# One inference step of a hybrid decoder: the prompt's compressed keys and values join the other key blocks

## Chip, cores and metric

The kernel runs on one core of a Trainium2 chip. The metric is the device time of one execution in microseconds (us); before the change it is 1101.69 us, the median of three runs (1101.4 to 1104.07). The engines are named as in the profile: PE (TensorE, matmuls) with PEld (its weight loads), DVE (VectorE), ACT (ScalarE), POOL (GpSimd), SP (SyncE, which issues most DMAs).

## The reference

One layer with two head groups is computed for a prompt of 1024 tokens and for 8 decode samples. An input projection (1024 to 4384 columns) feeds 4 mLSTM heads of 128 and 8 attention heads of 64 with 2 shared key/value heads. Each attention head has three branches, merged by gates. The change concerns the prompt's first branch, the compressed one, and the sum over all three:

```python
def nsa_prompt(qa, cmp_rows, slc_rows, win_rows, ga, cmp_params, rel_bias):
    kc = compress(cmp_rows, *cmp_params)            # 63 compressed keys and values per KV head
    o_c, imp = cmp_attend(q, kc, t_pos, rel_bias)   # softmax over the compressed keys
    ...
    o_w = window_prompt(q, win_rows, rel_bias)      # keys of the last 512 positions
    return gate_merge(ga, o_c, o_s, o_w)            # g0*o_c + g1*o_s + g2*o_w
```

`compress` takes windows of 32 positions with a step of 16: two halves of 16 positions, each times its half of `w1`, are added to a bias; GELU, then `w2`, for keys and for values. In the second branch the 16 selected blocks of 64 are all there are, so `o_s` runs over all earlier keys.

The output projection, a residual and a layer norm follow, and several caches and states are outputs too.

## The kernel before

Everything is emitted by generators ("lanes") with a rank. A planner (`Plan`, `Lanes`) keeps a modelled clock for each engine; at each turn the lane of lowest rank whose operands its model holds to be ready emits its next step. So the order of instructions on each engine is fixed when the program is built, and each engine works in that order. All of this is recorded through one helper, which is why every row of the profile has line L281; tiles tell the rows apart.

- Projections (`mm`): three float32r matmuls (`hh`x`wh`, `hl`x`wh`, `hh`x`wl`) per 128 input rows and 344 tokens. Their lane has the highest rank number, 9, so they fill PE wherever no other lane is ready.
- `kv_done` (L1158) takes a projected key or value tensor. For the compressed branch it copies it into `xtp`, with even positions on partitions 0 to 63 and odd ones on 64 to 127 (L1168 to 1178).
- `prompt_compress` (L1211): matmuls `sc<-xtp,w1f` read `xtp` through a view with a step of 8 elements, then GELU, then the compressed keys `kcp` and values `vcp`. The flag "pcmp" at its end starts the loads of the decode samples' selected keys (L1410) and is one of those that the attention waits for (L1968).
- `key_stacks` (L1832): keys are held as a float32r high part on 64 partitions and the remainder on the other 64. The selected keys go to `KS_` (tile `kst`, 1024 columns), the window's to `KW`, the compressed ones to `KC` (tile `kcs`).
- Attention works in 32 units: 2 KV heads x 8 query blocks of 128 x 2 pairs of heads. A unit with query block qb has nb = qb + 1 blocks of selected keys and min(nb, 5) of the window. `Unit.scores` (L2006) makes the logits of each of the unit's two heads in chunks of up to 512 columns (`score_chunks`, L1977): `qs` and `ql` are the high and low parts of the query, each a stationary operand for one matmul. In the first chunk the 64 compressed columns and the selected columns are two separate pairs of matmuls. DVE adds biases and finds minima, ACT takes exponentials into `pa` and `pw` (`pp` for nb up to 3; the compressed ones stand behind the window's in `pw`).
- `Unit.values` (L2104): blocks of 128 probabilities of both heads are scaled, transposed on PE (`tp`), copied from PSUM to a tile `pt` by ACT or DVE, and multiplied with the values (`oo<-pt,VT`), in groups of two blocks. A product has a stationary operand of 64 columns and goes to PSUM rows 0 to 63 for one head and 64 to 127 for the other. The compressed block is a group of its own, of 64 columns (`oo<-pt,vcp`). Products run LAG = 2 groups behind the transposes:

```python
                if len(pend) > LAG:
                    yield [pend[0][0]]
                    product(*pend.pop(0))
            while pend:
                yield [pend[0][0]]
                product(*pend.pop(0))
```

- Behind the last unit's values ("values") start the output gate, the samples' mLSTM (L1651) and the loads and splits of the output weights (L2273). The output projection comes last.

Of the kernel before, what the change touches and what calls it, by code (L numbers as in the profile page):

```python
# [9 lines left out]
F32R = mybir.dt.float32r  # L10
I32 = mybir.dt.int32
AF = mybir.ActivationFunctionType
ALU = mybir.AluOpType
# [314 lines left out]
def build(ctx, tc, I, O, dbg=None):  # L328
# [13 lines left out]
    def R(shape, name, dt=F32):  # L342
        return rp.tile(shape, dt, name=name, tag="R", bufs=NR)
# [811 lines left out]
    xtp = []  # L1155
    outs_kv = {0: ("cmp_p", "cmp_s"), 1: ("slc_p", "slc_s"), 2: ("win_p", None)}

    def kv_done(br, s, f):  # L1158
# [9 lines left out]
        if br == 0:  # L1168
            x = R([128, 2, 512], "xtp")
            fv = f[:, 0:SEQ].rearrange("p (n two) -> p two n", two=2)  # L1170
            for p2 in range(2):
                for kv in range(2):
                    o, i_ = x[64 * p2:64 * p2 + 64, kv], fv[64 * kv:64 * kv + 64, p2]
                    if kv:
                        S.activation(o, i_, AF.Copy)
                    else:
                        V.tensor_copy(o, i_)
            xtp.append(x)
# [29 lines left out]
    kcp = C([128, 2, 64], "kcp")  # L1208
    vcp = C([64, 2, 64], "vcp")

    def prompt_compress():  # L1211
# [5 lines left out]
        for c in range(2):  # L1217
            r = slice(64 * c, 64 * c + 64)
            ps = yield from bank("sc")
            xr = xtp[c].rearrange("p k (n a) -> p a k n", a=8)  # L1220
            for a in range(8):
                T.matmul(ps[:, 0:128], w1[c][:, a].rearrange("p j h -> p (j h)"), xr[:, a], start=(a == 0),
                         stop=(a == 7))
            S.activation(tm[r].rearrange("p k n -> p (k n)"), ps[64:128, 0:128], AF.Identity, bias=cst[r])
            V.tensor_tensor(x[r, :, 0:63], ps[0:64, 0:128].rearrange("p (k n) -> p k n", k=2)[:, :, 0:63],
                            tm[r, :, 1:64], op=ALU.add)
            yield
# [9 lines left out]
        for kv in range(2):  # L1237
            T.matmul(ps[0:64, 64 * kv:64 * kv + 64], x[64:128, kv], w2[64:128], start=True, stop=True)
        V.tensor_scalar(vcp.rearrange("p k e -> p (k e)"), ps[0:64, 0:128], 0.5, None, op0=ALU.mult)
        yield  # L1240
# [591 lines left out]
    def key_stacks(kv):  # L1832

        r = slice(64 * kv, 64 * kv + 64)
        KS_[kv], KW[kv] = [R([128, SEQ], "kst", F32R) for _ in range(2)]
        if not KC:
            KC.append(H([128, 2, 64], "kcs", F32R))
            stack(KC[0], kcp)
        VT[kv] = R([128, 2, 8, 64], "VT")
        near_bias(kv)  # L1840
        for t in range(2):
            m = slice(512 * t, 512 * t + 512)
            for i, k in enumerate((KS_[kv], KW[kv])):
# [3 lines left out]
                yield [a]  # L1847
                stack(k[:, m], a)
                if t == 0:
# [146 lines left out]
    class Unit:  # L1996
# [9 lines left out]
        def scores(self):  # L2006
# [9 lines left out]
            for g in range(2):  # L2016
# [13 lines left out]
                for i, (c0, c1) in enumerate(ca):  # L2030
                    ps = yield from bank("sc", True)
                    n = c1 - c0
                    s0 = max(c0, 64)
                    if i == 0:
                        product(ps[:, 0:64], KC[0][:, kv])
                    product(ps[:, s0 - c0:n], KS_[kv][:, s0 - 64:c1 - 64])
                    if i == 0:
# [66 lines left out]
        def values(self):  # L2104
# [6 lines left out]
            chunks += [(self.PW, c0, c1, 2, x) for x, (c0, c1) in enumerate(cw)]  # L2111
            groups = [[(self.PW, oc, 64, vcp[:, kv], 0)]]
            blocks = []
            for k, (P, c0, c1, br, x) in enumerate(chunks[1:], 1):
                for o in range(c0, c1, 128):
                    i = o // 128 + (nb - nbw if br == 2 else 0)
                    blocks.append((P, o, 128, VT[kv][:, br - 1, i], k))
            groups += [blocks[i:i + 2] for i in range(0, len(blocks), 2)]
            scaled = [0]
# [25 lines left out]
            for group in groups:  # L2145
# [9 lines left out]
                pend.append((pt, group))  # L2155
                if len(pend) > LAG:
                    yield [pend[0][0]]
                    product(*pend.pop(0))
            while pend:
                yield [pend[0][0]]  # L2160
                product(*pend.pop(0))
# [290 lines left out]
```

## Time and profile before

| | |
|---|---|
| median of three runs | 1101.69 us |
| the profiled execution | 1101.59 us, its span 1099.8 us |
| PE busy | 1009.0 us (92%), 7445 records |
| PEld busy | 884.3 us (80%) |
| DVE, ACT, POOL busy | 724.9, 525.2, 289.3 us |
| granted TensorE clock, mean | 0.966 of full speed |
| PE's share of the chain that ended last | 69%, DVE 17% |

How to read it: a float32 matmul or product appears as two records, a float32r one and a transpose as one. Matmuls are pipelined and their ends are modelled, so the length of a PE record is not what it costs; that is the distance to the next start, and for weight loads as well. "issue" is idle time in which an engine waited for nothing that the profile shows.

### The profile page before, as it was taken

How to read it: one execution, taken by the hardware profiler on the slowest of the kernel's cores; microseconds unless marked ns; L12 is line 12 of the kernel's file. 1: busy time of each engine (PE TensorE's matmuls, PEld its weight loads, DVE VectorE, ACT ScalarE, POOL GpSimd, SP SyncE). 2: the span in 40 equal slices, each digit the busy share in tenths (PEclk: the TensorE clock that was granted, in tenths of full speed). 3: DMA queues.
4: the chain of work that ended last, by engine and by line, in shares of the span. 5: the costliest groups of instructions: out<-in, count | busy, mean ns of one | idle time of the engine just before them, and what ended most of it. 6: DMA issues, size and time to landing. Idle time of an engine off the chain costs nothing.

```text
span 1099.8 us, 20348 instructions
## 1 busy us (share of the span) xinstructions
PE 1009.0 (92%) x7445; PEld 884.3 (80%) x7445; DVE 724.9 (66%) x2285; ACT 525.2 (48%) x1313; POOL 289.3 (26%) x363
## 2 busy tenths in 40 slices
PE   6898699999798999999999999999999999989991
PEld 5787698888675789889889888888888898867780
DVE  4678962252212446778787777878776757898996
ACT  4466662242243556666566676766774223231211
POOL 6315421111633111010113000111001533443463
PEclk9798899999899999999999999999999999989996
DMA  9953406504855753321002311011110515479512
GB/s 309 411 192 98 154 25 245 166 21 134 312 194 191 251 165 101 111 85 54 25 26 89 83 43 35 23 37 64 44 42 20 172 40 139 124 257 351 192 41 78
DMA packets 124750, 141.45 MB, mean 129 GB/s; under 512 B 21049, under 2 KB 102564, under 8 KB 124522
## 3 DMA queue, kind: packets, MB, share of 16 engines
q1 hardware_dynamic: 115434, 106.59, 30.9%
q0 software_dynamic: 9216, 33.56, 8.4%
q8 instruction: 59, 0.97, 0.4%
q14 instruction: 41, 0.34, 0.1%
HBM read 117.73 MB, written 28.15 MB: 133 GB/s over the span
## 4 chain that ended last, share of the span: by engine, by line
PE 69%; DVE 17%; issue 4%; DMA 3%; ACT 2%; POOL 2%; another core or an unknown queue 1%; SPq 1%; POOLq 0%; DVEq 0%; ACTq 0%
PE mm L281 30%; PE sc L281 17%; PE tp L281 13%; PE oo L281 8%; DMA wada<-in_w_ada 2%; DVE xr L281 2%; DVE rs_t L281 1%; SPq L281 1%; DVE lnst L281 1%; DVE smp L281 1%; DVE mixl L281 1%; DVE nd L281 1%; DVE tot L281 1%; DVE rs_y L281 1%
## 5 line engine op out<-in xcount | busy, mean ns | idle before, releaser
L281 PE MATMUL mm<-hh,wh 128*128 128x344 f32 (+1 forms) x840 | 285.9, 341 | 1.1 <-DVE pa L281 0.8
L281 PE MATMUL mm<-hl,wh 128*128 128x344 f32 (+1 forms) x840 | 269.8, 321 | 0.0
L281 PE MATMUL mm<-hh,wl 128*128 128x344 f32 x816 | 262.1, 321 | 0.0
L281 POOL TENSOR_TENSOR wl<-wf,wh 128x1024 fp32r<-128x1024 f32 (+1 forms) x35 | 83.0, 2372 | 498.7 <-ACT wh L281 343.6
L281 PEld LDWEIGHTS mm<-hh,wh 128*128 128x128 f32 (+1 forms) x840 | 158.3, 188 | 15.2 <-issue 10.8
L281 PEld LDWEIGHTS mm<-hl,wh 128*128 128x128 f32 (+1 forms) x840 | 158.5, 189 | 0.5
L281 PEld LDWEIGHTS mm<-hh,wl 128*128 128x128 f32 x816 | 154.7, 190 | 0.0
L281 PE MATMUL oo<-pt,VT 128*64 128x128 f32 x1056 | 78.0, 281 | 1.2 <-DVE pt L281 1.2
L281 ACT ACTIVATE pt<-tp 128x512 f32<-128x512 f32 (+2 forms) x88 | 46.6, 531 | 60.3 <-PE tp L281 59.6
L281 PE MATMUL sc<-kst,qs 128*128 128x384 f32 (+3 forms) x208 | 71.7, 350 | 0.6 <-ACT ti L281 0.5
L281 PEld LDWEIGHTS oo<-pt,VT 128*64 128x64 f32 x1056 | 55.7, 136 | 17.4 <-issue 10.2
L281 DVE COPY pt<-tp 128x512 f32<-128x512 f32 (+1 forms) x80 | 50.1, 635 | 25.8 <-PE tp L281 25.8
L281 PE MATMUL sc<-kst,ql 128*128 128x384 f32 (+3 forms) x208 | 63.8, 315 | 0.0
L281 ACT ACTIVATE pa<-pa,nbs 128x384 f32<-128x384 f32 (+1 forms) x88 | 51.0, 581 | 24.1 <-DVE pa L281 22.1
L281 ACT ACTIVATE xh<-tp 128x512 fp32r<-128x512 f32 x64 | 37.6, 595 | 47.6 <-PE tp L281 43.1
L281 ACT ACTIVATE pw<-pw,nbs 128x64 f32<-128x64 f32 (+2 forms) x112 | 54.6, 488 | 10.5 <-DVE nbs L281 5.4
L281 DVE TENSOR_TENSOR xl<-tp,xh 128x512 fp32r<-128x512 f32 x64 | 43.1, 683 | 21.3 <-ACT xh L281 16.8
L281 PE MATMUL tp<-KA,pgx 128*128 128x128 f32 x256 | 44.4, 301 | 6.7 <-issue 4.2
L281 PE MATMUL sc<-xl,w1h 128*128 128x256 f32 x128 | 39.6, 310 | 11.1 <-DVE xl L281 11.1
L281 PE MATMUL sc<-xh,w1h 128*128 128x256 f32 x128 | 44.5, 347 | 0.7 <-ACT xh L281 0.7
L281 ACT ACTIVATE ti<-sc,PKT 128x129 f32<-128x129 f32 x28 | 10.4, 371 | 70.2 <-DVE cx L281 70.2
L281 ACT ACTIVATE ktT<-tp 128x512 f32<-128x512 f32 x40 | 22.1, 596 | 44.8 <-PE tp L281 32.9
(509 smaller groups left out, 2377.7 us busy)
## 6 DMA issues: line engine op xcount, KB each, us to landing
wf<-in_w_in SPq DMA_DIRECT2D x34, 512.0 KB
wada<-in_w_ada SPq DMA_DIRECT2D x24, 512.0 KB
wof<-in_w_out SPq DMA_DIRECT2D x16, 512.0 KB
xt<-in_x_prompt SPq DMA_DIRECT2D x8, 512.0 KB
pgs<-in_cache_win_kv SPq DMA_DIRECT2D x8, 512.0 KB
qf<-qtd SPq DMA_DIRECT2D x32, 128.0 KB
mix<-mxd SPq DMA_DIRECT2D x16, 256.0 KB
mix<-gtd SPq DMA_DIRECT2D x16, 256.0 KB
```

The source lines that it names most:

```text
L281: return f(*a, **kw)
```

## The change

`xtp` is stored in the order in which it is read. `vcp` becomes 128 rows, with the values in the upper 64 and zeros below. The compressed keys stand in columns 0 to 63 of `kst` and the selected ones behind them; the last 56 of these, which don't fit in its 1032 columns, stay in `kcs`.

```diff
@@ kv_done
-            x = R([128, 2, 512], "xtp")
-            fv = f[:, 0:SEQ].rearrange("p (n two) -> p two n", two=2)
+            x = R([128, 8, 2, 64], "xtp")
+            fv = f[:, 0:SEQ].rearrange("p (n a two) -> p two a n", a=8, two=2)
...
-                    o, i_ = x[64 * p2:64 * p2 + 64, kv], fv[64 * kv:64 * kv + 64, p2]
+                    o, i_ = x[64 * p2:64 * p2 + 64, :, kv], fv[64 * kv:64 * kv + 64, p2]
@@ prompt_compress
-    vcp = C([64, 2, 64], "vcp")
+    vcp = C([128, 2, 64], "vcp")
...
-            xr = xtp[c].rearrange("p k (n a) -> p a k n", a=8)
+            xr = xtp[c].rearrange("p a k n -> p a (k n)")
...
-            T.matmul(ps[0:64, 64 * kv:64 * kv + 64], x[64:128, kv], w2[64:128], start=True, stop=True)
-        V.tensor_scalar(vcp.rearrange("p k e -> p (k e)"), ps[0:64, 0:128], 0.5, None, op0=ALU.mult)
+            T.matmul(ps[64:128, 64 * kv:64 * kv + 64], x[64:128, kv], w2[64:128], start=True, stop=True)
+
+        V.memset(vcp[0:64], 0.0)
+        V.tensor_scalar(vcp[64:128].rearrange("p k e -> p (k e)"), ps[64:128, 0:128], 0.5, None, op0=ALU.mult)
@@ key_stacks
-        KS_[kv], KW[kv] = [R([128, SEQ], "kst", F32R) for _ in range(2)]
+        KS_[kv], KW[kv] = R([128, NT], "kst", F32R), R([128, SEQ], "kst", F32R)
         if not KC:
-            KC.append(H([128, 2, 64], "kcs", F32R))
-            stack(KC[0], kcp)
+            KC.append(H([128, 2, SEQ + 64 - NT], "kcs", F32R))
+        stack(KS_[kv][:, 0:64], kcp[:, kv])
...
-                stack(k[:, m], a)
+                if i == 0:
+                    o = 64 + 512 * t
+                    n = min(512, NT - o)
+                    stack(k[:, o:o + n], a[:, 0:n])
+                    if n < 512:
+                        stack(KC[0][:, kv], a[:, n:512])
+                else:
+                    stack(k[:, m], a)
@@ Unit.scores
-                    if i == 0:
-                        product(ps[:, 0:64], KC[0][:, kv])
-                    product(ps[:, s0 - c0:n], KS_[kv][:, s0 - 64:c1 - 64])
+                    e = min(c1, NT)
+                    product(ps[:, 0:e - c0], KS_[kv][:, c0:e])
+                    if c1 > e:
+                        product(ps[:, e - c0:n], KC[0][:, kv])
@@ Unit.values
-            groups = [[(self.PW, oc, 64, vcp[:, kv], 0)]]
-            blocks = []
+            blocks = [(self.PW, oc - 64, 128, vcp[:, kv], 0)]
...
-            groups += [blocks[i:i + 2] for i in range(0, len(blocks), 2)]
+            groups = [blocks[i:i + 2] for i in range(0, len(blocks), 2)]
...
-                if len(pend) > LAG:
-                    yield [pend[0][0]]
+                if len(pend) > LAG + 1:
+                    yield [pend[1][0]]
                     product(*pend.pop(0))
+                    product(*pend.pop(0))
+            yield [x[0] for x in pend]
             while pend:
-                yield [pend[0][0]]
                 product(*pend.pop(0))
```

The compressed block is now 128 columns wide: its lower 64 are the last columns of the window's block beside it, which meet the zeros of `vcp`. It is the first of the unit's blocks, and these go in groups of two throughout. Products start when four groups are pending and then go two groups at a time; at the end all that is left goes together.

The order on PE in a unit's values, for a unit with nb = 6 (12 blocks). `pa` and `pw` are probabilities, `nd` belongs to the mLSTM. Before:

```order
L281 MATMUL oo<-pt,vcp 64x128 x2
L281 MATMUL tp<-KA,pa 128x128 x4
L281 MATMUL oo<-pt,VT 64x128 x4
L281 MATMUL tp<-KA,pw 128x128 x4
L281 MATMUL oo<-pt,VT 64x128 x4
L281 MATMUL tp<-KA,pw 128x128 x4
L281 MATMUL oo<-pt,VT 64x128 x4
L281 MATMUL tp<-KA,pw 128x128 x2
L281 MATMUL oo<-pt,VT 64x128 x10
L281 MATMUL tp<-KA,nd 128x128 x4
```

And after, for a unit of the same size, with the mLSTM's (`vx`, `cx`) and the next scores (`kst`) behind it:

```order
L281 MATMUL tp<-KA,pw 128x128 x2
L281 MATMUL oo<-pt,vcp 64x128 x2
L281 MATMUL oo<-pt,VT 64x128 x6
L281 MATMUL tp<-KA,pw 128x128 x8
L281 MATMUL oo<-pt,VT 64x128 x16
L281 MATMUL sc<-vx,kw 128x129
L281 MATMUL sc<-cx,qm 128x129
L281 MATMUL sc<-vx,wt 128x129
L281 MATMUL sc<-kst,qs 128x448
L281 MATMUL sc<-kst,ql 128x448
```

The same 24 products stand in two runs where there were five.

The order on PE in the scores of one head with nb = 8 (`vm` belongs to the mLSTM). Before:

```order
L281 MATMUL sc<-kcs,qs 128x64
L281 MATMUL sc<-kcs,ql 128x64
L281 MATMUL sc<-kst,qs 128x384
L281 MATMUL sc<-kst,ql 128x384
L281 MATMUL tp<-KA,pw 64x128 x2
L281 MATMUL tp<-KA,pa 128x128 x4
L281 MATMUL tp<-KA,vm 128x128 x4
L281 MATMUL sc<-kst,qs 128x384
L281 MATMUL sc<-kst,ql 128x384
L281 MATMUL sc<-kst,qs 128x256
L281 MATMUL sc<-kst,ql 128x256
```

After:

```order
L281 MATMUL sc<-kst,qs 128x448
L281 MATMUL sc<-kst,ql 128x448
L281 MATMUL tp<-KA,pw 128x128 x2
L281 MATMUL tp<-KA,pa 128x128 x2
L281 MATMUL sc<-kst,qs 128x384
L281 MATMUL sc<-kst,ql 128x384
L281 MATMUL sc<-kst,qs 128x200
L281 MATMUL sc<-kst,ql 128x200
L281 MATMUL sc<-kcs,qs 128x56
L281 MATMUL sc<-kcs,ql 128x56
```

The pair of 64 columns is gone from the first chunk, which has 448 now, and in this largest size a pair of 56 columns has come at the end of the third; the transposes of 64 columns (`tp<-KA,pw 64x128`) are gone too.

## Rows read from the trace of the kernel before

**Rows 1.** The windows view over four stretches of the span: the stretch in us, its length, busy us and instructions of PE, PEld, DVE, ACT and POOL, the granted clock, the DMA share and GB/s.

```profile
260.00:385.00 125.00, 108.65 (x866) 87.94 (x866) 34.41 (x73) 46.61 (x90) 39.87 (x36) 0.96 0.64 216
385.00:850.00 465.00, 456.99 (x3755) 403.38 (x3754) 343.37 (x1441) 302.18 (x911) 62.56 (x145) 1.00 0.21 61
850.00:975.00 125.00, 116.88 (x785) 108.71 (x784) 91.81 (x237) 32.76 (x67) 49.55 (x64) 0.99 0.44 131
975.00:1100.00 125.00, 96.88 (x444) 75.86 (x442) 109.22 (x199) 24.09 (x29) 57.45 (x28) 0.89 0.54 177
```

**Rows 2.** The waits of PE between 385 and 850 us: who waited for whom, us in total, times, the longest; the first, second and last of eight.

```profile
PE tp L281 <- DVE pp L281: 2.9, 3, 1.4
PE oo L281 <- DVE pt L281: 1.2, 1, 1.2
...
PE tp L281 <- DVE kw L281: 0.2, 1, 0.2
```

**Rows 3.** The same view for PEld: the four with "issue".

```profile
PEld oo L281 <- issue: 15.0, 86, 0.4
PEld tp L281 <- issue: 10.6, 54, 1.5
PEld mm L281 <- issue: 6.7, 39, 0.2
PEld sc L281 <- issue: 4.3, 21, 0.3
```

**Rows 4.** PE in order of time, in the attention: start in us, length, engine, line, operation, tiles, shape of the stationary operand, shape of what is streamed, records merged. Left out are the `ql` matmuls, each of the width of the `qs` before it, and one more pair of 256.

```profile
657.86 0.34 PE L281 MATMUL sc<-kst,qs 128*128 128x384 f32 x1
...
658.21 0.28 PE L281 MATMUL sc<-kst,qs 128*128 128x256 f32 x1
...
658.44 0.34 PE L281 MATMUL sc<-kst,qs 128*128 128x384 f32 x1
...
659.12 0.66 PE L281 MATMUL oo<-pt,VT 128*64 128x128 f32 x8
659.71 0.66 PE L281 MATMUL tp<-KA,pw 128*128 128x128 f32 x4
660.30 0.66 PE L281 MATMUL oo<-pt,VT 128*64 128x128 f32 x8
660.89 0.43 PE L281 MATMUL mm<-hh,wh 128*128 128x344 f32 x1
```

**Rows 5.** The same view at two more places: a long run of products, and six transposes (the two of the compressed block, 64 columns wide, come first; the form shown is theirs).

```profile
665.32 1.31 PE L281 MATMUL oo<-pt,VT 128*64 128x128 f32 x20
666.56 0.43 PE L281 MATMUL mm<-hh,wh 128*128 128x344 f32 x1
...
847.02 0.82 PE L281 MATMUL tp<-KA,pp 128*64 128x128 f32 x6
847.59 0.40 PE L281 MATMUL mm<-hh,wh 128*128 128x344 f32 x1
```

**Rows 6.** The chain of waits between 255 and 300 us, in order of time: start, us, what. `sc` x16 are the matmuls on `xtp`.

```profile
259.07 0.44 PE tp L281 x4
259.51 0.95 PE mm L281 x6
260.46 3.72 PE sc L281 x16
...
265.57 3.73 PE sc L281 x16
...
275.78 12.50 another core or an unknown queue
```

**Rows 7.** The tile `kcs`: count, shortest/median/longest in ns, first and last start in us, form. The rows for `ql` are as many.

```profile
L281 PE MATMUL sc<-kcs,qs x64: 191/193/277, 385.8 to 832.6; 128*128 128x64 f32 x64
...
L281 ACT ACTIVATE kcs<-kcp x1: 298/298/298, 361.6 to 361.6; 128x128 fp32r<-128x128 f32 x1
L281 DVE TENSOR_TENSOR kcs<-kcp,kcs x1: 2377/2377/2377, 361.9 to 361.9; 64x128 fp32r<-64x128 f32 x1
```

**Rows 8.** PEld in order of time, at the first head's scores.

```profile
385.80 0.19 PEld L281 LDWEIGHTS sc<-kcs,ql 128*128 128x128 f32 x1
385.91 0.19 PEld L281 LDWEIGHTS sc<-kst,qs 128*128 128x128 f32 x1
386.02 0.19 PEld L281 LDWEIGHTS sc<-kst,ql 128*128 128x128 f32 x1
```

**Rows 9.** PE in order of time, at float32 matmuls of the mLSTM whose streamed operand lies in adjacent columns.

```profile
853.04 1.05 PE L281 MATMUL sc<-qm,km 128*128 128x128 f32 x8
853.85 0.41 PE L281 MATMUL mm<-hh,wh 128*128 128x344 f32 x1
```

**Rows 10.** The tiles `tp`, `xtp` and `oo`, columns as in rows 7: the copies to `pt`, the copies to `xtp`, and the products.

```profile
L281 ACT ACTIVATE pt<-tp x88: 363/593/600, 420.1 to 847.4; 128x512 f32<-128x512 f32 x63, 64x256 f32<-64x256 f32 x18, 128x256 f32<-128x256 f32 x7
L281 DVE COPY pt<-tp x80: 406/684/693, 430.4 to 847.9; 128x512 f32<-128x512 f32 x65, 64x256 f32<-64x256 f32 x14, 128x256 f32<-128x256 f32 x1
...
L281 ACT ACTIVATE xtp<-kvf x4: 659/668/672, 231.8 to 247.1; 64x512 f32<-64x512 f32 x4
L281 DVE COPY xtp<-kvf x4: 406/420/422, 234.0 to 246.8; 64x512 f32<-64x512 f32 x4
...
L281 PE MATMUL oo<-pt,VT x1056: 272/273/324, 423.9 to 849.5; 128*64 128x128 f32 x176
```

## Prediction

> **What bounds the kernel now.** I read the stretches first, then who waits for whom inside the attention, then the order of time on TensorE (PE). Four stretches, cut by what PE does [rows 1]: up to 385 us projections and the decode samples' keys; 385 to 850 us the prompt's attention, with projection matmuls as filler; 850 to 975 us the rest of the projections with the mLSTM; then the output projection. In the attention PE is busy 457.0 of 465 us, DVE 343.4, ACT 302.2, at a granted clock of 1.00. All that PE waits there for another engine is eight groups of 2.9 down to 0.2 us, 7.8 us together [rows 2]. So PE's instruction stream sets the pace of 465 us, and any time taken out of it should come off. After 975 us it is different: DVE is busy 109.2 of 125 us and PE 96.9.
>
> PE's busy time hides something, though. The weight loads (PEld) stand idle with nothing to wait for ("issue") 86 times before a product `oo`, 54 times before a transpose `tp`, 39 before a projection `mm` and 21 before a score `sc`: 36.6 us for 200 times, 0.18 us each [rows 3]. The order of time shows where. A run of eight `oo` records (two blocks of keys) takes 0.59 us to the next start, one of twenty takes 1.24 [rows 4, 5]. The twelve more cost 0.65, so a record costs 0.054, eight cost 0.43, and 0.16 us belongs to the run, however long. Four transposes followed by a product take 0.59 us [rows 4]; in the chain of waits four take 0.44 [rows 6]; 0.15 more. One excursion into the value products so costs about 0.16 + 0.15 = 0.31 us beside its work. What differs is the shape: a product's stationary operand has 64 columns and writes 64 output rows, all around it work on 128.
>
> **The change part by part.**
>
> *Value products in twos.* In the order of the two programs I counted the uninterrupted runs of rows that write `oo` from `pt`: 120 before, 63 after. The rule in the code gives nearly that: a unit with G groups makes one run per group beyond two, and one flush (108 over all units; other lanes split some); now one per two groups beyond three, and a flush (60). 57 fewer excursions at 0.31 are 17.7 us. Bounds: 0.16 us if only one side of a run is really paid (9.1), and twice the mean idle of 0.183 (20.9). I take 0.31, which is read from the runs themselves. The compressed keys' products also stop being a shape of their own (64 rows instead of 128), which I count at nothing beyond the runs.
>
> *Scores.* There are 64 head units (32 units of 2 heads), and each loses one narrow matmul for `qs` and one for `ql` [rows 7]. In the weight loads everything up to 128 columns follows at 0.11 us [rows 8]: 128 x 0.11 = 14.1 us. The first chunk of each head becomes 64 columns wider. Two matmuls of 384 columns take 0.35 us and two of 256 take 0.23 [rows 4], so 64 columns are 0.03 us; 112 matmuls pay it (3.4 us), and the 16 that go from 128 to 192 columns stay at the 0.11. The eight heads with eight blocks get two more matmuls of 56 columns, because the keys end at column 1032: 16 x 0.11 = 1.8, less 0.1 for their 256 that become 200. Net 14.1 - 3.4 - 1.7 = 9.0 us. Bounds: 12.4 if the wider ones cost nothing more; 5.6 if each of the 112 pays the whole step of 0.06 us between 256 and 384 columns.
>
> *Compress.* Two sets of sixteen matmul records read `xtp` with a step of 32 bytes and take 3.72 and 3.73 us on the chain [rows 6]; eight records of the same size that read adjacent columns take 0.81 us [rows 9], so sixteen take 1.62. 2 x 2.1 = 4.2 us. Both stand on the chain, and behind them come the gathers of the samples' keys (12.5 us of a queue, same rows), which start when `kcp` and `vcp` are written; they move up with it. Bounds 0 and 4.2; I take 4.2. The other side of this edit are the eight copies that fill `xtp`, 0.42 us on DVE and 0.67 on ACT now [rows 10]. They read with a step of 64 bytes instead of 8. The nearest row for a strided read is PE's own, 3.72 against 1.62, a factor of 2.3: 4 x (0.55 + 0.87) = 5.7 us more on two engines under full projection work. The cover is the `mm` filler; the bounds are 0 and 5.7, and I take 0.
>
> The Trainium skill has a rule on this, in "SBUF — State Buffer", the note on SBUF lines in the section on the DMA port swizzle: reads that leave a 16-byte line at each element lose bandwidth. By it `xtp` read contiguously gains, as the factor shows, and the copies, now at 64 bytes, lose, which speaks against the change; this is the second rival below.
>
> *What is added.* One memset of half of `vcp`; three more pieces for the key stacks in all (an ACT and a DVE instruction each; the widest seen, for `kcp`, took 0.30 and 2.38 us [rows 7]) in front of or under filler work: 0 to 5 us, taken as 0. The compressed transposes become 128 wide. In the trace six transposes of which two are 64 wide go in 0.57 us [rows 5], like full ones, so nothing changes. Eight copies of `pt` fewer, 0.59 or 0.68 us each [rows 10], on engines that are not waited for: 0. In units of up to three blocks the first transposes now also wait for the scaling of the window's columns: 12 units with up to 0.4 us; queued behind them is the filler, which comes first where they aren't ready. I take 1 us.
>
> *What is late next.* PE walks through the attention some 6% faster, against the same DVE and ACT work: 343 of about 438 us is 78%. The 7.8 us of waits [rows 2] should grow; I take 3 us, bounds 0 and 8. In the order, 480 projection matmuls stand behind the last product, before it was 510; the 30 at 0.158 us (0.95 us for six, [rows 6]), 4.7 us, go ahead of it. In total PE work this is nothing, but the last stretches have idle PE time (116.9 of 125 busy), so part of it isn't won back: 1.5 us, bounds 0 and 4.7.
>
> **Sum.** -17.7 - 9.0 - 4.2 + 1 + 3 + 1.5 = -25.4 us. The profiled execution took 1101.59 us (span 1099.8), which is the median of the runs (1101.69) within 0.1; 1101.6 - 25.4 = 1076. What follows the attention starts at the flag of the last unit (gate, samples' mLSTM, output weights), so it moves with it.
>
> The Trainium skill states in "TensorEngine Tiling (Array Packing)", Key Properties, that changing the tiling mode drains the engine. Our products' boundaries fit that. Taken by the letter it holds for the 64-column transposes too, and the change removes 32 runs of these, another 10 us: 1066. The row of six transposes shows no such cost.
>
> **Rivals.**
> - *64-column transposes pay as well*: 32 runs x 0.31 = 9.9 us more won, 1066. Against it: the 0.57 us for six [rows 5]. Chance 5%.
> - *The copies into `xtp` are slow and uncovered*: 5.7 us later, 1082. For it: the factor of 2.3 on PE. Against it: DVE and ACT are behind `mm` work there, which doesn't read `xtp`. Chance 5%.
> - *DVE or ACT become the bound* in the attention. If half of its 26.7 us is lost to waits (in place of the 3 us), it is -13.3 - 4.2 + 2.5 = -15 us, 1087. For it: DVE ends the longest of PE's present waits. Against it: all of these are 7.8 us. Chance 12%.
> - *The excursion's cost is of each block, not of the run*, so putting runs together saves nothing: -9.0 - 4.2 + 5.5 = -7.7 us, 1094. Against it: 1.24 us for twenty records, 0.59 for eight. Chance 5%.
> - *The change doesn't reach the end*: what follows the attention takes up what it wins, and the kernel stays at 1100. For it: PE has idle time there, 8.1 and 28.1 of 125 us [rows 1]. Against it: all of it waits for the last unit's flag or for projections. Chance 4%.
> - *Slower*: PE works in order, and a flush now needs the copies of up to three groups at once. If each of the 63 runs waits for its last copy, 0.6 us [rows 10], that is 38 us: -25.4 + 38 = +12.6, 1114. It decides from 25.4 / 63 = 0.40 us per run. For it: such a wait was there once, 1.2 us [rows 2]. Against it: by the spacings above, each group's products stand at least 1.1 us of PE work behind its last transpose in the new order, median 2.8 (before 0.7 and 2.0). Chance 4%.
>
> **How the numbers follow.** The forecast has 65%; its own ends are 20.9, 12.4 and 4.2 us won with no loss (1064), and 9.1 in place of 17.7 for the runs (1085). The range 1064 to 1091 takes in the first three rivals with room above the third, and leaves out the last three, 13%, and the forecast's outer ends. A measurement of this kernel can't tell less than about 0.3% (3.3 us) from no change: faster 92% (the forecast and the first four rivals), same 4%, slower 4%.
>
> **What would show it.** Right: the narrow `kcs` matmuls are 16 of 56 columns, 0.11 us apart; issue idle of PEld before `oo` falls from 86 times to about half; `sc<-xtp` sixteen records in about 1.6 us; the last product `oo` at about 827 us instead of 849 [rows 10] (-17.7 - 9.0 - 4.2 + 1 + 3 and the 4.7 of projections that now come ahead), and some 247 us behind it instead of 250. Wrong: PE waiting for `pt` copies or for `pa`, `pw` from DVE by more than 10 us in the attention; PEld idle as often as before; or a last product that comes early and an end that doesn't.

## The result, and the profile after

The changed kernel takes 1058.7 us (median of 4 runs, 1058.3 to 1061.3) beside 1101.55 us for the kernel before on the same chip (1099.3 to 1104.1): a ratio of 0.9615, 95% interval 0.9589 to 0.9641, or 42.9 us won. The forecast was 1076, with a range from 1064 to 1091. The direction was right; the gain was 1.7 times the forecast and the time lies 5 us below the range.

The windows view of after, cut by the same events as [rows 1]; the first stretch starts with the matmuls on `xtp`, as there:

```profile
258.00:385.00 127.00, 113.11 (x918) 91.41 (x918) 36.61 (x82) 50.11 (x96) 42.80 (x43) 0.95 0.71 234
385.00:820.00 435.00, 426.76 (x3637) 394.72 (x3636) 339.10 (x1426) 303.06 (x919) 60.28 (x138) 1.00 0.21 60
820.00:937.00 117.00, 110.71 (x736) 103.29 (x737) 86.59 (x230) 32.41 (x67) 47.93 (x63) 0.97 0.45 133
937.00:1057.00 120.00, 94.36 (x440) 73.28 (x438) 104.79 (x197) 24.32 (x29) 56.54 (x29) 0.94 0.55 185
```

The attention went from 465 to 435 us, and PE's idle time in it stayed at 8 us. The stage behind it went from 125 to 117, the last from 125 to 120. Nothing was won ahead of the first score, which starts at 384.8 us instead of 385.8.

The waits of PE in the attention, to be read against [rows 2] (the three longest):

```profile
PE tp L281 <- DVE pa L281: 2.5, 3, 1.6
PE tp L281 <- DVE pw L281: 2.2, 2, 1.6
PE tp L281 <- DVE tot L281: 0.8, 1, 0.8
```

All groups together are 7.7 us; before they were 7.8. PE goes through the stage faster, and nobody makes it wait longer. The idle time of the weight loads with nothing to wait for, to be read against [rows 3]:

```profile
PEld oo L281 <- issue: 9.0, 45, 0.4
PEld tp L281 <- issue: 4.6, 21, 0.7
...
PEld mm L281 <- issue: 3.6, 21, 0.2
...
PEld sc L281 <- issue: 2.8, 16, 0.2
```

That is 103 times and 20.0 us; it was 200 times and 36.6 us. The tiles `kcs`, `xtp` and `oo`, to be read against [rows 7, 10]:

```profile
L281 PE MATMUL sc<-kcs,qs x8: 207/208/210, 577.3 to 629.4; 128*128 128x56 f32 x8
...
L281 PE MATMUL sc<-xtp,w1f x32: 270/275/275, 257.6 to 262.4; 128*128 128x128 f32 x32
...
L281 ACT ACTIVATE xtp<-kvf x4: 1076/1096/1106, 229.3 to 244.8; 64x512 f32<-64x512 f32 x4
...
L281 DVE COPY xtp<-kvf x4: 574/596/608, 231.5 to 244.3; 64x512 f32<-64x512 f32 x4
...
L281 PE MATMUL oo<-pt,VT x1056: 272/273/324, 422.4 to 819.7; 128*64 128x128 f32 x176
```

The narrow score matmuls are down to eight (and eight for `ql`), the copies that fill `xtp` got longer, and the last product is at 819.7 us instead of 849.5. Sixteen compress matmuls take 1.78 us to the next start instead of 3.72 [rows 6]:

```profile
257.61 1.95 PE L281 MATMUL sc<-xtp,w1f 128*128 128x128 f32 x16
259.39 0.60 PE L281 MATMUL tp<-KA,kvf 128*128 128x128 f32 x4
```

To compare kernels whose matmuls overlap, I put on each matmul the time from its start to the start of the next one on PE, without the idle gap that the trace shows between them, and sum by kind. "Trio" is small transposes (`tp` of `pp`, `pa`, `pw`), products (`oo` from `pt`) and scores (`kst`, `kcs`) over the whole kernel. "Tail" is the time from the end of the last matmul to the end of the span. All in us, from one profiled execution each; the last column is counted in the order of PE's instructions. Some expectations below give the trio as 273 us in before and 243.8 in after: these count the transposes of `pgx` too, some 30 us, which stand ahead of the compress matmuls and are not part of the change. G's 33 us, further below, rests on the same count; without `pgx` it is 31.9.

| kernel | span | trio | `xtp` | idle of PE | tail | output stage (first output matmul to end) | runs of products |
|---|---|---|---|---|---|---|---|
| before | 1099.8 | 241.5 | 7.4 | 61.8 | 24.6 | 124.5 | 120 |
| after | 1057.2 | 213.4 | 3.6 | 60.3 | 18.3 | 120.5 | 63 |
| e_compress | 1092.0 | 241.6 | 3.6 | 59.0 | 24.5 | 124.5 | 120 |
| e_twos | 1073.1 | 228.1 | 7.4 | 55.8 | 24.3 | 124.7 | 69 |
| e_scores | 1104.7 | 233.5 | 7.4 | 79.6 | 15.7 | 141.2 | 127 |
| e_join | 1097.3 | 240.4 | 7.4 | 64.9 | 16.5 | 128.9 | 107 |
| a_noTwos | 1075.8 | 228.3 | 3.6 | 59.1 | 25.0 | 125.1 | 107 |
| a_noScores | 1077.5 | 222.3 | 3.6 | 63.2 | 24.1 | 124.1 | 62 |
| a_noCompress | 1063.5 | 213.8 | 7.4 | 61.3 | 16.7 | 122.0 | 63 |
| after_again | 1052.5 | 213.2 | 3.6 | 58.5 | 18.3 | 120.6 | 63 |
| a_threes | 1057.2 | 208.6 | 3.6 | 60.3 | 16.7 | 121.1 | 48 |

From before to after the trio falls by 28.1 us and `xtp` by 3.8: 31.9 of the 42.6 us between the spans. The experiments ask whether these 31.9 us belong to the parts as forecast, and where the other eleven come from.

### The profile page after: what moved, and what is told of

Same layout as the page of the kernel before. It is cut to its first block, busy times and chain, and to the rows that moved or that the text cites. A ratio compares the mean times of both kernels' runs of the same rounds, so it can differ in the third digit from the quotient of the medians.

```text
span 1057.2 us, 20105 instructions
## 1 busy us (share of the span) xinstructions
PE 974.2 (92%) x7333; PEld 869.8 (82%) x7333; DVE 713.9 (68%) x2271; ACT 531.3 (50%) x1326; POOL 288.2 (27%) x363
## 4 chain that ended last, share of the span: by engine, by line
PE 71%; DVE 14%; DMA 3%; issue 3%; ACT 2%; POOL 2%; another core or an unknown queue 1%; SPq 1%; POOLq 0%; DVEq 0%; ACTq 0%
PE mm L281 33%; PE sc L281 17%; PE tp L281 13%; PE oo L281 8%; DMA wada<-in_w_ada 2%; DVE rs_t L281 1%; SPq L281 1%; DVE xr L281 1%; DVE lnst L281 1%; DVE smp L281 1%; DVE pa L281 1%; POOL rs_t L281 1%; POOL wol L281 1%; DVE rs_y L281 1%
## 5 line engine op out<-in xcount | busy, mean ns | idle before, releaser
L281 PE MATMUL oo<-pt,VT 128*64 128x128 f32 x1056 | 69.9, 276 | 0.0
L281 PE MATMUL sc<-kst,qs 128*128 128x448 f32 (+6 forms) x208 | 68.7, 340 | 0.3 <-DVE pt L281 0.3
L281 PE MATMUL sc<-kst,ql 128*128 128x448 f32 (+6 forms) x208 | 64.9, 323 | 0.0
L281 DVE COPY pt<-tp 128x512 f32<-128x512 f32 (+1 forms) x86 | 54.1, 639 | 15.2 <-PE tp L281 14.9
L281 ACT ACTIVATE pt<-tp 128x512 f32<-128x512 f32 (+1 forms) x74 | 40.9, 565 | 45.3 <-PE tp L281 45.0
L281 PEld LDWEIGHTS oo<-pt,VT 128*64 128x64 f32 x1056 | 58.1, 137 | 5.8 <-issue 4.1
L281 ACT ACTIVATE pa<-pa,nbs 128x384 f32<-128x384 f32 (+1 forms) x88 | 51.0, 581 | 16.0 <-DVE pa L281 12.6
L281 ACT ACTIVATE pp<-pp,nbs 128x64 f32<-128x64 f32 (+3 forms) x72 | 32.2, 449 | 22.4 <-DVE nbs L281 20.6
L281 ACT ACTIVATE ti<-sc,PKT 128x129 f32<-128x129 f32 x28 | 10.3, 369 | 64.9 <-DVE cx L281 64.9
```

The lines of the kernel that those rows point to most:

```text
L281: return f(*a, **kw)
```

## The experiments

Three theories stood first. W: each part is worth the PE time that it takes away. P: the planner, which orders all engines by its own costs, makes another order of each edit, and that order moves the idle time. (The planner also chooses the engine of a copy by its clocks, so another order moves some copies between ACT, DVE and POOL.) S: one part is worth far more than its PE time.

**One part alone, on before** (one set of runs; before took 1097.0 us in it).

*e_compress*: only the layout of `xtp`; the order stays that of before, except that six projections and four transposes change places beside the copies into `xtp`.

```diff
-            x = R([128, 2, 512], "xtp")
+            x = R([128, 8, 2, 64], "xtp")
...
-            xr = xtp[c].rearrange("p k (n a) -> p a k n", a=8)
+            xr = xtp[c].rearrange("p a k n -> p a (k n)")
```

> The kernel before with the compress input stored contiguously and nothing else; the order on PE is that of before. Theory W (every part is worth the PE time that it takes out of the stream, and all of it reaches the end): 4.2 us faster, 1097.4, the two sets of sixteen records in 1.6 us each. Theory P (the 17 us beyond the forecast come from how the planner's new order falls, in idle time outside the attention): the same 4.2, since the order doesn't move. Theory S (one part of the change is worth far more than its PE time): if it is this one, 10 us or more.

Measured: 1094.7 us, ratio 0.9956 (0.9920 to 0.9993): 1 to 9 us won by the interval, so the total can't tell more than that it fell. `xtp` fell by 3.8 us. As W.

*e_twos*: only the products in twos.

```diff
-                if len(pend) > LAG:
-                    yield [pend[0][0]]
+                if len(pend) > LAG + 1:
+                    yield [pend[1][0]]
+                    product(*pend.pop(0))
                     product(*pend.pop(0))
...
```

> The kernel before with products two groups at a time and nothing else: 69 runs of products instead of 120. W: 51 x 0.31 = 15.8 us faster, 1085.8. P: off from 15.8 by 5 us or more either way, with the difference in the idle time of PE behind the last product. S: 25 us or more if it is this part.

Measured: 1075.9 us, ratio 0.9820 (0.9760 to 0.9879), about 20 us won with 51 runs fewer. The trio fell by 13.4. One cost that only this kernel has is seen on PE in order of time, here and then in after:

```profile
422.76 0.44 PE L281 MATMUL oo<-pt,vcp 64*64 64x128 f32 x4
423.13 0.66 PE L281 MATMUL oo<-pt,VT 128*64 128x128 f32 x8
```

```profile
422.10 0.44 PE L281 MATMUL oo<-pt,vcp 128*64 128x128 f32 x4
422.37 0.61 PE L281 MATMUL oo<-pt,VT 128*64 128x128 f32 x8
```

From the compressed block's four products to the next start it is 0.37 us while their weights are 64 rows by 64, and 0.27 once they are 128 by 64 like the others. With 32 such places that is 3.2 us which the twos win only together with the joined block. With them it would be 16.6 us for 51 runs, 0.33 each; without, 0.26.

*e_scores*: only the compressed keys at the front of the key stacks.

```diff
...
-                    if i == 0:
-                        product(ps[:, 0:64], KC[0][:, kv])
-                    product(ps[:, s0 - c0:n], KS_[kv][:, s0 - 64:c1 - 64])
+                    e = min(c1, NT)
+                    product(ps[:, 0:e - c0], KS_[kv][:, c0:e])
+                    if c1 > e:
+                        product(ps[:, e - c0:n], KC[0][:, kv])
```

> The kernel before with the compressed keys in front of the selected ones and nothing else: 112 fewer score matmuls (9.2 us), but 127 runs of products instead of 120 (2.2 us). W: 7.0 us faster, 1094.6. P: off from 7.0 by 5 us or more, in the idle time behind the last product. S: 17 us or more if it is this part.

Measured: 1103.4 us, ratio 1.0060 (1.0031 to 1.0088): slower by 0.6%, although the trio fell by 8.0 us. The planner had put 144 more projection matmuls into the attention and left 366 behind it instead of 510. The windows of the output stage and of its first 20 us, and PE's waits in the stage:

```profile
963.50:1104.70 141.20, 100.54 (x442) 76.83 (x440) 112.17 (x198) 25.25 (x30) 67.60 (x35) 0.86 0.50 167
963.50:983.50 20.00, 3.97 (x12) 1.97 (x10) 18.68 (x28) 6.84 (x8) 9.78 (x5) 0.68 0.89 311
```

```profile
PE sc L281 <- ACT woh L281: 8.9, 2, 7.6
PE sc L281 <- DVE wol L281: 7.1, 1, 7.1
PE sc L281 <- ACT mixh L281: 4.1, 1, 4.1
```

PE came to the output projection before its weights were split: 16 us of waits for `woh` and `wol`, at a DMA share of 0.89, and a clock of 0.68 there. So W holds for the work in the trio and P for the time.

*e_join*: only the compressed block as half of a pair, with 128-column transposes.

```diff
...
-            groups = [[(self.PW, oc, 64, vcp[:, kv], 0)]]
-            blocks = []
+            blocks = [(self.PW, oc - 64, 128, vcp[:, kv], 0)]
...
```

> The kernel before with the compressed block joined to the other value blocks and nothing else: 107 runs of products instead of 120, no transposes of 64 columns, no product of 64 rows. W: 13 x 0.31 = 4.0 us faster, 1097.6. If the 32 runs of 64-column transposes had each cost a switch as well: 13.9 us, 1087.7. P: off from 4.0 by 5 us or more, in the idle time behind the last product. S: 15 us or more.

Measured: 1098.0 us, ratio 1.0000 (0.9969 to 1.0032). The trio fell by 1.1 us, less than W's 4.0: small transposes and products fell by 3.8, and the scores, the same matmuls, took 2.7 more; the granted clock was 0.988 over this attention and 0.996 over before's. The output stage grew by 4.4. Had the 64-column transposes cost a switch each, 9.9 us more would have gone from transposes and products; that rival falls.

By the medians the four alone sum to 16 us (2.4 + 21.2 - 6.3 - 1.0), against 42.9 for the whole.

**One part undone, from after** (one set; before 1101.3 us, after again 1059.2).

*a_noTwos* and *a_noScores* are the inverse of the diffs of e_twos and e_scores, *a_noCompress* of that of e_compress.

> After, with the value products one group at a time again. 107 runs of products instead of 63. W (each part is worth the PE time that it takes away, wherever it stands): 44 runs more at 0.31 to 0.35 us each are +13.6 to +15.4 us, so 1072 to 1074 us. P (the planner's new order, through idle time of TensorE behind the last product and in the output stage, makes up the rest of the gain): the time differs from W's by more than 5 us either way, and the difference stands in the lengths of the last two stages (117.0 and 120.5 us in after), not in the attention net of the projection matmuls.

Measured: 1075.7 us, 16.5 above after; the trio 14.9 above it, for 44 runs: 0.34 us each. The weight loads idle before `oo` again:

```profile
PEld oo L281 <- issue: 13.2, 73, 0.4
```

The time is 1 us above W's upper bound, and its size fits W. But P's place for it is seen as well: these 14.9 us stand in the attention, and the stage is only 8.0 longer, as 3.1 us less filler and 1.8 less idle time stand in it; the last two stages are 4.6 us longer each (121.6 and 125.1).

> After, with the prompt's compressed block scored apart again (128 narrow score matmuls of 64 columns, 16 of 56 gone). W: +9.2 us of score work less about 0.3 for one run of products fewer, +8.9, so about 1067.6 us. P: more than 5 us off that, with the difference in the last two stages.

Measured: 1078.8 us, 19.6 above after. The trio is 8.9 above after, as W has it; the rest is not: the output stage is 3.6 us longer, the stage ahead of it 4.3 (121.3 against 117.0), and PE's idle time in the attention is 11.6 us instead of 8.2. That is P.

> After, with the compress input strided again; the order of all engines stays that of after. W: the sixteen matmul pairs on xtp go from 0.11 to 0.23 us a record, +3.8 to +4.2 us, about 1063 us, all of it in the stage before the first score. P has nothing to act with here, since the order is the same: it gives the same +4 us. If it costs less than 2 us, the stage before the first score is bounded by another engine and the compress part wasn't worth its term.

Measured: 1063.3 us, 4.1 above after, with 3.8 in `xtp`. As W. This kernel has after's order behind the compress matmuls, and its output stage is within 1.5 us of after's.

> After unchanged, a second profile. If the 3.4 us less before the first projection matmul and the 4.0 us less in the output stage belong to the change, they come again within 1 us (116.1 and 120.5 us). If they are the variation of one execution, either stage goes back toward 119.5 and 124.5 us, and that much of the 42.9 us is not the change's.

Measured: 1059.2 us, ratio 0.9624 (0.9602 to 0.9646). The output stage came again at 120.6 us. The start did not: 117.5 us to the first projection matmul, and 119.5 in a_noCompress with the same order, against 116.1 in after and 119.5 in before. So the shorter output stage goes with the order, and the 3.4 us at the start are the variation of one execution. The granted clock is a small part of that stage's 4 us at most: it was 0.943 over it in after, 0.924 in the second profile at the same length, and 0.897 in a_noCompress, where the stage took 122.0 us; before has 0.890 and 124.5.

Undone one by one, the three parts give back 40 us. The joined block was not undone by itself. The scores are worth more inside after (19.6 us) than alone (-6.3), with nearly the same work taken away (8.9 and 8.0 us in the trio); the difference lies in stages that the planner's order fills. For the twos it is the other way (16.5 and 21.2).

**The price of a run, and the tail.**

*a_threes*: three groups of products in a row, 48 runs.

```diff
-                if len(pend) > LAG + 1:
-                    yield [pend[1][0]]
-                    product(*pend.pop(0))
-                    product(*pend.pop(0))
+                if len(pend) > LAG + 2:
+                    yield [pend[2][0]]
+                    for _ in range(3):
+                        product(*pend.pop(0))
```

> After, with the products of three groups in a row instead of two: 48 runs of products instead of 63, the same matmuls. X (a run of products among other work costs a fixed price): small transposes, products and scores together take 243.8 us of TensorE in after; 15 runs fewer at 0.35 us take 5.3 us off, about 238.5 us, and the whole is 3 to 6 us faster than after, about 1054 us. Y (a longer row of products holds copies and banks back): that sum falls as in X, but TensorE's idle time in the attention grows from 8 us by as much or more, and the whole is at 1058 us or above.

Measured: 1061.0 us, ratio 0.9654 (0.9633 to 0.9675), no gain over after (0.9615 and 0.9624). The trio fell by 4.8 us, 0.32 for each of 15 runs, with no more idle time in the attention (7.6 us); so X holds there, and the total is as Y has it, without Y's cause. But here are attention and the stage behind it, of a_threes and of after:

```profile
383.90:812.10 428.20, 420.61 (x3622) 393.02 (x3620) 344.62 (x1427) 298.03 (x915) 59.13 (x138) 1.00 0.21 61
812.10:936.00 123.90, 114.66 (x756) 107.13 (x751) 87.77 (x233) 32.85 (x67) 47.58 (x63) 0.94 0.42 128
```

```profile
384.80:819.70 434.90, 426.66 (x3638) 394.77 (x3636) 339.02 (x1425) 303.26 (x919) 60.28 (x138) 1.00 0.21 60
819.70:936.70 117.00, 110.71 (x741) 103.17 (x736) 86.57 (x230) 32.28 (x66) 47.93 (x63) 0.97 0.45 134
```

The stage behind the attention took all of it back (123.9 against 117.0 us): six more projections, 2.9 us more idle time, and a lower clock in this execution (0.94 against 0.97).

*b_noSmp* and *a_noSmp*: before and after without the samples' last layer norm.

```diff
-        yield from finish(ys, slice(32, 40), O["y_sample"].rearrange("b t d -> (b t) d"))
+        yield [ys]
+        dma(O["y_sample"].rearrange("b t d -> (b t) d"), ys)
```

> Before, with the decode samples' last layer norm left out (the unnormed rows are stored). D (the end of the kernel is set by VectorE's backlog in the output stage: 24.6 us from the last matmul to the end in before, 18.3 in after): some 12 us of VectorE's work in that stage are gone, the time behind the last matmul falls to 12 to 17 us, and the whole is 7 to 12 us faster than before, 1089 to 1094 us. E (the end is set by TensorE's matmuls and the last tile's own chain): the time behind the last matmul stays at 24 us and the whole within 2 us of before.

> After, with the decode samples' last layer norm left out in the same way. D: the time behind the last matmul falls from 18.3 to 12 to 17 us; the whole is 2 to 6 us faster, less than the same edit gives in before, and the distance between the two kernels shrinks from 42 to some 36 us, which is what their matmuls and transposes differ by. E: nothing falls, and the distance stays at 42 us.

Measured: 1096.7 and 1054.6 us, beside 1098.8 for before (ratios 0.9986, 0.9955 to 1.0018, and 0.9598, 0.9576 to 0.9620). The tail fell as D says, from 24.6 to 15.7 us and from 18.3 to 15.2. But the output stage lost only 3.7 and 3.9 us (120.8 and 116.6): in before the matmuls ended 5.2 us later in it, which took most of the gain. The distance of the two kernels stayed at 42.0 us. So VectorE's backlog does lengthen the tail, while the after kernel's shorter output stage doesn't come from where the samples' norm lies. D's numbers for before and for the distance fell.

**The order alone.** One number of the planner (0.2 in both kernels), set to 0.3 and to 0.15 in both. PE's instructions are the same and come in another order; on ACT, DVE and POOL 49 to 95 of each kernel's instructions stand on another of the three. "The same instructions" in the expectations holds for PE.

```diff
-SLACK = 0.2
+SLACK = 0.3
```

> Before, with one number of the planner changed (how far ahead of TensorE's clock a step may be planned, 0.2 to 0.3): 990 projection matmuls inside the attention and 618 behind the last product, instead of 1110 and 510; the same instructions in another order. If order alone moves the end, small transposes, products and scores stay at 273 us within 1.5 and the time behind the last matmul or TensorE's idle time (61.8 us) changes by 3 us or more. If order plays no part, all of them stay and the time is within 3 us of before.

> Before with the planner's allowance at 0.15 in place of 0.2: 54 projection matmuls more ahead of the attention, 54 more in it, 402 instead of 510 behind the last product; the same instructions. If the order is worth up to 5 us either way in either kernel: 1094 to 1106 us. If it is worth nothing: within 2 us of before.

> After with the allowance at 0.15: 65 runs of products, 432 projection matmuls behind the last product. G (33 us of the gain are TensorE work taken away in any order, the other 9 or so are this one order against that one): the distance to the kernel before with the same 0.15 lies between 28 and 38 us. H (the whole 42 us belong to the change in any order): it is 40 us or more, as at 0.2.

> After with the allowance at 0.3: 61 runs of products, 498 projection matmuls behind the last product. G: the distance to the kernel before with the same 0.3 (0.9962 of before's time) lies between 28 and 38 us, so 1059 to 1069 us. H: 40 us or more, 1057 us or below.

> Before with the allowance at 0.3, once more, so that the pair at 0.3 and the pair at 0.2 are taken in one set of runs. G: 36 +- 4 us from here to after with the same 0.3, and 40 to 44 us from before to after at 0.2. H: both distances agree within 3 us.

> After with the allowance at 0.3. G: 36 +- 4 us below the kernel before with 0.3. H: 40 us or more below it. A time under that of after in this set by more than 3 us would make 0.3 the better setting for the changed kernel.

> After unchanged, in the same set. 40 to 44 us below before, as in the two earlier sets; if it lies outside, the set and not the order moves the distance, and the pair at 0.3 says less than G and H want of it.

b_slack took 1096.9 us in the set with before at 1098.8, as if order played no part. Its parts say otherwise: the trio is 9.2 us longer (250.7) and the tail 7.9 shorter (16.7). What the order costs and what it gives back nearly cancel.

In the last two sets all kernels were about 20 us faster (before 1079.5 and 1078.9), so only distances within a set are used:

| setting | before's instructions | after's instructions | apart |
|---|---|---|---|
| 0.15 | b_s15 1092.0 | a_s15 1062.3 | 29.7 |
| 0.2 | before 1078.9 | after_third 1040.6 | 38.3 |
| 0.3 | b_slack_again 1079.9 | a_slack_again 1042.0 | 37.9 |

At 0.2 the two earlier sets gave 42.9 and 42.1; the 38.3 is 34.5 to 41.1 by its interval. With four runs of each, the 29.7 is known to some 7 us. Neither G nor H holds as written. G has 28 to 38 us at 0.15 and 0.3, which came (29.7 and 37.9), and 40 to 44 at 0.2 in the same set, which didn't. H has one distance in every order: 0.2 and 0.3 agree, but lie under its 40, and 0.15 is far from it. Order alone is worth 12.6 us in before (0.15 against 0.2, one set; 6 to 17 by the interval), and 21.9 in after's instructions (a_slack took 1040.4 us beside a_s15); I had allowed 5.

The trio is 27.9 us apart at 0.15 (245.0 and 217.1), 28.1 at 0.2 and 34.3 at 0.3 (248.3 and 214.0). The 6 us more at 0.3 are in part the clock: 8.2 us of b_slack_again's trio ran while the granted clock was low, in these two windows of its attention, and none of a_slack_again's:

```profile
380.00:388.00 8.00, 5.51 (x20) 5.27 (x21) 4.91 (x28) 3.05 (x13) 0.00 (x0) 0.57 0.14 35
436.00:444.00 8.00, 8.00 (x50) 6.91 (x50) 5.18 (x23) 4.75 (x16) 0.11 (x1) 0.59 0.42 144
```

At 0.15 the changed kernel loses part of its gain to waits in its attention:

```profile
372.10:829.60 457.50, 441.35 (x3724) 403.19 (x3722) 356.32 (x1482) 303.90 (x925) 67.85 (x174) 1.00 0.21 62
```

```profile
PE tp L281 <- ACT kx L281: 3.9, 2, 2.4
PE tp L281 <- ACT pp L281: 3.3, 3, 1.5
PE tp L281 <- DVE pp L281: 3.0, 2, 1.8
```

Its idle PE time there is 16 us, after's is 8. The trio and `xtp` together fall by 32 to 38 us in every order tried; what the whole kernel adds to that lies between -2 and +11 us.

## Why the prediction was right and wrong

*Products in twos, -17.7, and scores, -9.0*: right. In the attention itself products and small transposes fell by 18.4 us (83.4 + 75.8 to 74.2 + 66.6) and scores by 9.7 (82.3 to 72.6): 28.1 for 26.7. The run of products as the unit of cost is shown by three kernels (0.34 us a run in a_noTwos, 0.32 in a_threes, 0.26 in e_twos, or 0.33 with the 3.2 us of the compressed block's shape; forecast 0.31). The joined block's products "at nothing beyond the runs" held for this change; their shape costs its 3.2 us only where they stand in one run with the others and aren't joined, as in e_twos.

*Compress, -4.2*: right, 3.8. The copies into `xtp` cost 0.43 us (ACT) and 0.18 us (DVE) more each, 2.4 us for all eight, under cover: from the first projection to the compress matmuls it is 140.8 us in before, 141.5 and 140.3 in the two profiles of after. That rival's mechanism is real, its price is not on the path.

*The transposes that wait for the window (+1) and more waits in the attention (+3)*: wrong. PE's idle time there was 8.0 and is 8.2 us. DVE and ACT had 339 and 303 us of work in 435, and that was room enough.

*What is left over at the end (+1.5)*: wrong, and it is the largest single miss. The forecast had 247 us behind the last product; it is 237.5, before 250.3. Of the 12.8, 5.3 are the 30 projections that went ahead (rightly seen), 1.6 other work that went with them, 1.8 idle time and 3.9 the output stage. The last goes with the planner's order, and so, it seems, does the idle time (8.0 to 8.5 us in before, e_compress and b_noSmp, 6.3 to 7.3 in after, its two repeats, a_noCompress and a_noSmp). At 0.2 the output stage is 124.1 to 125.1 us in before, e_compress, e_twos, a_noTwos and a_noScores, and 120.4 to 122.0 in after, its two repeats, a_noCompress and a_threes. At 0.3 it is the other way: 122.0 us for b_slack_again, 126.6 for a_slack_again. The prediction also misread the last stretch: it put PE's 28.1 us of idle time there down to waits for the last unit's flag or for projections, but 24.6 of them are the tail behind the last matmul, in which DVE works. PE's own waits in that stage are 3.3 us in before.

*Not in the sum at all*: work that the new order moved ahead of the first score. Sixteen `ktT` matmuls (3.7 us) and more projections left the stages behind it. In the stage before, 127.2 us long and 125.5 before the change, work grew by 4.2 us net of the 3.8 that `xtp` gave back, while PE's idle time there was 2.4 us less (16.3 and 13.9). That 2.4 may be the variation of one execution: e_compress and b_noSmp, with before's order, have 13.3 and 12.6. In the changed kernel the gain of the compress part is thus not seen where I said, as an earlier first score, but behind it.

In sum, of the 17 us between forecast and result, about 11 are the three positive terms (+5.5 forecast; +0.2, -1.8 and -3.9 measured), 1.0 the work itself (1.4 more in the attention, 0.4 less in compress), and the rest what the profiled execution was faster by up to the compress matmuls (2.7, and not the change's) and the smaller idle time behind them (2.4). The step that failed is the three positive terms, and above all "what is late next": the new order was treated as something that can only lose, with bounds from 0 up, where kernels with the same PE instructions in other orders differ by 12.6 and 21.9 us, and the gain of this change itself moved between 29.7 and 42.9. The bounds of an order must reach to both sides of 0; I would now give it 10 us either way.

*Of what would show it*: 16 narrow `kcs` matmuls, half the idle times before `oo`, and sixteen `xtp` records in 1.8 us came as written or nearly (forecast 1.6). The last product came 7 us earlier than forecast. Nothing of the list for "wrong" came.

*The rivals*: the 64-column transposes (e_join), the cost by block instead of by run (a_noTwos, a_threes), DVE or ACT as the bound and the flush that waits (PE's waits of 7.7 us) were not there. That the change doesn't reach the end did come about in another kernel: e_scores and a_threes won in the trio and lost it behind the attention.

What stays open is why after's order has the shorter output stage at 0.2. The samples' norm is excluded, and the granted clock explains 1.5 of its 4 us at most; the order of the other VectorE work there wasn't tried. So it is shown that 6 to 11 us of the gain at 0.2 lie beyond the work taken from the trio and `xtp`, and that this part moves with the order (-2 at 0.15, 0 at 0.3), but not which step of the order brings it.

## What to carry to other kernels

Look for the price of changing the shape of work on PE in the weight loads' idle time without a releaser, and pay it once per run: group what has the same shape. Where a planner sets the order, an edit is worth its PE time plus or minus what another order does; run the same instructions at two or three settings of the planner before a few us are put down to an edit. And a part that loses alone can be worth more than its PE time in the whole: the scores here lost 6.3 us alone and were worth 19.6 in after.

## What the runs showed of the hardware

Behind one wait of 3 us the granted clock fell in one execution and not in another. Here are three windows of 4 us at the start of the output stage, of after and of a_noCompress, with the same order there and the same wait of PE for `wol` (2.9 us):

```profile
936.70:940.70 4.00, 2.83 (x12) 1.77 (x10) 3.93 (x7) 2.12 (x4) 1.25 (x1) 1.00 0.48 195
940.70:944.70 4.00, 1.86 (x8) 1.54 (x9) 4.00 (x3) 0.98 (x1) 4.00 (x2) 1.00 0.79 230
944.70:948.70 4.00, 4.00 (x19) 3.24 (x18) 3.87 (x12) 1.06 (x1) 1.76 (x2) 1.00 0.81 292
```

```profile
941.60:945.60 4.00, 2.79 (x12) 1.73 (x10) 3.93 (x7) 2.17 (x4) 1.30 (x1) 1.00 0.49 198
945.60:949.60 4.00, 1.90 (x5) 1.52 (x6) 4.00 (x3) 0.93 (x1) 4.00 (x2) 0.59 0.81 243
949.60:953.60 4.00, 4.00 (x12) 3.14 (x11) 3.87 (x12) 1.06 (x1) 1.67 (x2) 0.55 0.86 290
```

With the granted clock near its lower level (0.5 is 1.2 GHz), PE starts 12 matmuls in a window in which it otherwise starts 19.

The 20 us between the sets of runs lie ahead of the first score, most of them in one stage. Here it is in after and in after_third, the same kernel:

```profile
257.60:384.80 127.20, 113.31 (x921) 91.61 (x919) 36.41 (x82) 49.91 (x95) 42.80 (x43) 0.95 0.71 235
```

```profile
253.40:365.30 111.90, 107.87 (x921) 88.04 (x920) 37.36 (x82) 49.76 (x95) 44.14 (x43) 1.00 0.79 267
```

```profile
PE tp L281 <- DVE kx L281: 8.7, 2, 8.0
```

```profile
PE tp L281 <- DVE kx L281: 2.4, 1, 2.4
```

PE waits 8.7 us for `kx`, the gathered keys, in the one and 2.4 in the other, at 235 and 267 GB/s. Of the 15.3 us, 9.9 are idle time of PE, and 5.4 its busy time, at a granted clock of 0.95 and 1.00. Why the loads were faster, no run shows. From the first score to the end both take 672.4 us.

And a VectorE instruction on a single column can be ten times as long beside a GpSimd one: in before, `rs_t` on 128x1 takes 0.23 us and then 2.25, while GpSimd's addition to `xr` runs from 1072.75 to 1075.16 us:

```profile
1072.46 0.23 DVE L281 SCALAR_TENSOR_TENSOR rs_t<-rs_y,rs_v 128x1 f32<-128x1 f32 x1
...
1072.92 2.25 DVE L281 SCALAR_TENSOR_TENSOR rs_t<-rs_y,rs_v 128x1 f32<-128x1 f32 x1
```

```profile
1072.75 2.41 POOL L281 TENSOR_TENSOR xr<-xr,lb 128x1024 f32<-128x1024 f32 x1
```

The slowed instruction ends with GpSimd's. It doesn't happen each time: in before it is the only one over 1 us of 51 on 128x1 that overlap a GpSimd instruction, in after there are four of 48, and none of the 404 and 407 without one takes over 0.23 us. This chain of small instructions is on the way to the last rows of the output.
